# Feed-forward layer in two passes with a one-level Strassen input product

## The chip, the cores and the metric

The kernel runs on one core of a Trainium2 chip: TensorE (PE) for matrix products, VectorE (DVE), ScalarE (ACT) and GpSimd (POOL) for elementwise work, SyncE (SP) for issuing transfers between the off-chip memory and the on-chip buffers. The metric is the device time of one execution in microseconds (us), as the median of several runs.

## The reference

One layer of a hybrid diffusion backbone on 256 context tokens and 2048 latent tokens of width 1024, in float32. A mixing sublayer (differential attention, grouped-query attention, a bidirectional state-space scan) comes first, then a SwiGLU feed-forward sublayer; each ends in a layer norm. Only the second sublayer is changed. What matters of it:

```python
def swiglu(h, w_in, w_out):
    g, u = jnp.split(jnp.einsum('btd,df->btf', h, w_in), 2, axis=-1)
    return jnp.einsum('btf,fd->btd', jax.nn.silu(g) * u, w_out)
...
f = swiglu(x * (1 + scale2) + shift2, lp['w_ffn_in'], lp['w_ffn_out'])
x = layer_norm(ALPHA * x + gate2 * f, lp['ln_g'][1], lp['ln_b'][1])
```

The hidden width is 2816, which is 22 features of 128, each with a gate part g and an up part u.

## The kernel before

The stages run one after the other: modulation and input projections, state-space scans, attention, the output projection of the mixing sublayer (class `OutProj`), then the feed-forward layer (class `Ffn`, from L1536). For the engines PE, ACT, DVE and POOL, and in the last two stages for SP too, the order of the instructions is the order in which the program emits them. Every product is formed from operands split in two rounded parts, a high one and a low one (a float32r copy on ACT, the rest by a subtraction), as high x high + high x low + low x high: three matmuls for each 128 rows of the contraction.

`Ffn` works on three blocks of 768 tokens (18 tiles of 128). While the output projection does its last tiles, `inputs(0)` fetches and splits the first block's modulated rows, transposed, a 128-feature slice at a time (L1559 to L1565). For each block the 22 features go in four parts (`PARTS`). `hidden` forms a feature: for g, then for u, a piece of 128 x 1024 weights is loaded by SP (L1590), copied on ACT (L1593) and subtracted on POOL (L1594, the first ones on DVE), and for each half of 384 tokens 24 matmuls go into one bank (L1632 to L1634, tile pf). ACT takes the SiLU of g, DVE multiplies by u out of the bank, and ACT and DVE split the result into hh and hl (L1637 to L1640). After the features of a part, `out` multiplies them with their rows of the output weights, split by ACT and DVE (L1604, L1605), into six banks for each half of the 1024 columns (L1645 to L1647, tile fo), and `collect` adds the banks to facc (L1652, L1654). `normed` finishes a block beside the next block's features: gate on POOL (L1678), residual and statistics on DVE (L1680, L1683), scale on ACT (L1692), weight on DVE (L1693) and bias on POOL (L1695). The last part of the last block goes tile by tile (`last_out`, tile fl).

## Time and profile before

| what | value |
|---|---|
| median of 3 runs (lowest, highest) | 3869.7 us (3869.44, 3875.66) |
| the profiled execution: its span | 3868.3 us |
| mean granted TensorE clock | 0.974 of 2.4 GHz |
| busy DVE, ACT, POOL over the span | 2025.6, 1628.3, 1700.2 us |
| first matmul of the feed-forward stage, start | 2194.01 us |
| moved by DMA over the span | 318.67 MB, mean 82 GB/s |

The profiled execution is known by its span, from its first to its last instruction; the times of runs are those of the whole execution on the device. Durations of matmuls in a trace are modelled and overlap, so the distance between two starts is what one of them costs in a stream.

### The profile page before, as it was taken

To read this page: it belongs to the slowest core of one execution; us is meant where nothing else is said; L and a number is where in the kernel's file an instruction comes from. 1 tells how busy PE (TensorE), PEld (TensorE's weight loads), DVE (VectorE), ACT (ScalarE), POOL (GpSimd) and SP (SyncE) were. 2 spreads that over 40 slices of the span, in tenths; PEclk is the share of its full clock that TensorE was granted. 3 is DMA by queue.
4 is the path that set the end of the run, shared out by engine and by line. 5 is a ranking of instruction groups with operands and counts; after the bars stand their busy time and mean duration, and the time that the engine had idled before them with its cause. 6 is when DMAs were issued, how large, how long until landed. Compare 5 with 4: busy or idle time off the path is not lost.

```text
span 3868.3 us, 53596 instructions
## 1 busy us (share of the span) xinstructions
PE 3698.6 (96%) x20970; PEld 3006.8 (78%) x20970; DVE 2025.6 (52%) x3710; ACT 1628.3 (42%) x2802; POOL 1700.2 (44%) x1315
## 2 busy tenths in 40 slices
PE   6999899979999999999999999999999999999997
PEld 4878799965555554454478899999989999999996
DVE  3776666658888987667556521211611222611134
ACT  4555555538888883444434322122322122322212
POOL 3443267738888884445534422112422111611233
PEclk8999799989999999999999999999999999999999
DMA  5111244453310112011045511112321112311121
GB/s 195 46 52 39 91 128 124 122 163 117 88 39 20 42 39 65 14 33 36 14 161 178 181 63 68 66 58 72 129 91 60 68 64 97 133 60 58 68 101 52
DMA packets 214476, 318.67 MB, mean 82 GB/s; under 512 B 38632, under 2 KB 145032, under 8 KB 209616
## 3 DMA queue, kind: packets, MB, share of 16 engines
q1 hardware_dynamic: 194544, 295.49, 23.4%
q10 hardware_dynamic: 17232, 11.09, 1.0%
q0 software_dynamic: 2448, 8.67, 0.6%
q8 instruction: 165, 2.70, 0.3%
q14 instruction: 87, 0.71, 0.1%
HBM read 247.68 MB, written 67.52 MB: 81 GB/s over the span
## 4 chain that ended last, share of the span: by engine, by line
PE 46%; DVE 2%; POOL 1%; ACT 1%; issue 0%; DMA 0%; POOLq 0%; SPq 0%; ACTq 0%; DVEq 0%
PE pf L1634 9%; PE pf L1633 9%; PE pf L1632 9%; PE fo L1647 4%; PE fo L1646 4%; PE fo L1645 4%; PE opo L1440 2%; PE opo L1439 2%; PE opo L1438 2%; PE mpt L1430 0%; DVE facc L1680 0%; PE npt L1478 0%; POOL wi L1594 0%; DVE facc L1693 0%; DMA wir<-in_wfi 0%
## 5 line engine op out<-in xcount | busy, mean ns | idle before, releaser
L1594 POOL TENSOR_TENSOR wi<-wir,wi 128x1024 fp32r<-128x1024 f32 x128 | 313.7, 2451 | 1118.1 <-ACT wi L1593 1095.2
L1634 PE MATMUL pf<-fxh,wi 128*128 128x384 f32 x2112 | 708.3, 335 | 8.2 <-POOL wi L1594 6.9
L1632 PE MATMUL pf<-fxh,wi 128*128 128x384 f32 x2112 | 707.7, 335 | 1.3 <-ACT wi L1593 1.3
L1633 PE MATMUL pf<-fxl,wi 128*128 128x384 f32 x2112 | 707.5, 335 | 0.0
L1638 DVE TENSOR_TENSOR sg<-pf,sg 128x384 f32<-128x384 f32 x132 | 73.4, 556 | 768.2 <-PE pf L1634 761.5
L1176 DVE TENSOR_SCALAR_CACHE_REDUCE e<-ps 128x1024 f32<-128x1024 f32 (+1 forms) x384 | 393.1, 1040 | 66.2 <-PE ps L1171 64.5
L1634 PEld LDWEIGHTS pf<-fxh,wi 128*128 128x128 f32 x2112 | 397.9, 188 | 10.4 <-POOL wi L1594 8.5
L1632 PEld LDWEIGHTS pf<-fxh,wi 128*128 128x128 f32 x2112 | 398.0, 188 | 2.2 <-ACT wi L1593 1.7
L1633 PEld LDWEIGHTS pf<-fxl,wi 128*128 128x128 f32 x2112 | 397.8, 188 | 0.4
L1187 ACT ACTIVATE e<-e,nb 128x2560 f32<-128x2560 f32 x128 | 311.0, 2429 | 41.1 <-DVE nb L1181 41.1
L1593 ACT ACTIVATE wi<-wir 128x1024 fp32r<-128x1024 f32 x132 | 138.9, 1053 | 438.5 <-issue 341.8
L1209 POOL TENSOR_TENSOR e<-e,e 128x512 f32<-128x512 f32 x254 | 296.6, 1168 | 21.2
L1647 PE MATMUL fo<-wfh,hl 128*128 128x512 f32 x762 | 296.7, 389 | 0.0
L1646 PE MATMUL fo<-wfl,hh 128*128 128x512 f32 x762 | 296.6, 389 | 0.0
L1645 PE MATMUL fo<-wfh,hh 128*128 128x512 f32 x762 | 296.4, 389 | 0.0
L957 DVE TENSOR_REDUCE gmx<-gm 128x1 f32<-128x512 f32 (+1 forms) x304 | 214.2, 715 | 118.0 <-PE gm L956 115.5
L1171 PE MATMUL ps<-dk,dq 96*128 96x512 f32 x640 | 241.5, 460 | 28.8 <-DVE e L1176 16.8
L997 POOL TENSOR_TENSOR gag<-gag,ge 128x1024 f32<-128x1024 f32 x80 | 208.3, 2604 | 127.4 <-ACT ge L981 126.3
L1605 DVE TENSOR_TENSOR wfl<-wfr,wfh 128x512 fp32r<-128x512 f32 x127 | 90.2, 711 | 328.7 <-ACT wfh L1604 328.7
L981 ACT ACTIVATE ge<-gs 128x1024 f32<-128x1024 f32 x160 | 163.7, 1024 | 217.5 <-PE gs L979 213.5
L1639 ACT ACTIVATE hh<-sg 128x384 fp32r<-128x384 f32 x132 | 69.5, 526 | 433.7 <-DVE sg L1638 431.7
L1604 ACT ACTIVATE wfh<-wfr 128x512 fp32r<-128x512 f32 x127 | 79.9, 630 | 356.0 <-PE fo L1647 345.3
(433 smaller groups left out, 8088.3 us busy)
## 6 DMA issues: line engine op xcount, KB each, us to landing
wir<-in_wfi SPq DMA_DIRECT2D x132, 512.0 KB, 3.5
wfr<-in_wfo SPq DMA_DIRECT2D x132, 256.0 KB, 2.6
wada<-in_w_ada SPq DMA_DIRECT2D x24, 1024.0 KB, 7.2
yr<-in_xT SPq DMA_DIRECT2D x18, 512.0 KB, 3.8
stk_d<-sod SPq DMA_DIRECT2D x18, 512.0 KB, 3.4
mt<-mix_d SPq DMA_DIRECT2D x18, 512.0 KB, 4.8
xt<-in_xtok SPq DMA_DIRECT2D x18, 512.0 KB, 5.6
fxr<-x2T_d SPq DMA_DIRECT2D x24, 384.0 KB, 5.4
```

The costliest lines, as they stand in the source:

```text
L957: V.tensor_reduce(mx[:, 4 * r + q, i:i + 1], ps[:, 0:w], AX.X, ALU.max)
L1171: PE.matmul(ps[:, 512 * c:512 * c + 512], Q[0:96, m, qs], K[0:96, m, k0:k0 + 512], start=True, stop=True)
L1176: V.tensor_scalar(self.e[m][:, k0:k0 + w], ps[:, c:c + w], dscale, -3.4e38, ALU.mult, ALU.max, accum_out=mx[:, m, seen[m]:seen[m] + 1])
L1187: S.activation(self.e[m], self.e[m], AF.Exp, bias=self.nb[:, m:m + 1], accum_out=self.l[:, m:m + 1])
L1209: G.tensor_tensor(e0[:, a:b], e0[:, a:b], e1[:, a:b], ALU.add)
L1594: (G if f > 1 or blk else V).tensor_tensor(wl, raw, wh, ALU.subtract)
L1632: PE.matmul(o, wh[:, k], self.xh[:, k, cs], start=(k == 0), stop=False)
L1633: PE.matmul(o, wh[:, k], self.xl[:, k, cs], start=False, stop=False)
L1634: PE.matmul(o, wl[:, k], self.xh[:, k, cs], start=False, stop=(k == 7))
L1645: PE.matmul(po, hh[:, n, ts_], w[0], start=start, stop=False)
L1646: PE.matmul(po, hh[:, n, ts_], w[1], start=False, stop=False)
L1647: PE.matmul(po, hl[:, n, ts_], w[0], start=False, stop=stop)
```

## The change

The input product goes through all blocks first, and writes its result to memory (`h_d`, 22 x 128 x 2304); a second pass reads it back for the output product.

First pass (`first`), blocks of 768 tokens. The weights of a feature are a 2 x 2 matrix of blocks (g and u by two halves of the 1024 contraction rows), the tokens' rows another (two halves of the contraction by two halves of 384 tokens). Seven products of sums of such blocks, of four 128-row steps each, take the place of eight: products 1 (a, operand 11), 2 (a, 21), 5 (c, t1), 6 (d, t2), 7 (c, t3), 4 (b, t4), 3 (d, 22) in this order; t1 to t4 are the operand sums, c and d hold the weight sums. The sums that put the products together are formed on DVE from the banks and on POOL between SBUF tiles (`features`). Weight sums are formed on POOL in the first block (DVE for feature 0), stored in `ws_d` and loaded from there in the later blocks; a feature's weights are prepared beside the feature before it. The operand sums of the first block are formed on DVE (`start` beside the output projection, `rest` in feature 0), those of the later blocks on POOL beside the first block's features (`sums_of`, four sums a block), stored in `xc_d`. At a block's last feature the seven operands of the next are split (`inputs`).

Second pass (`second`): five groups of 4, 4, 4, 3 and 3 token tiles. For each group and each of the 22 features a piece holds 128 x 1024 output weights and the group's h (`pieces`), fetched three ahead and split by ACT and DVE into one of seven buffers; all 1024 columns of a tile accumulate over the 22 features in two banks. The last four features go tile by tile, and each tile is then gated, added to the residual and normalised (`added`, `normed`) beside the next group. The buffers of both passes are laid out anew; docstrings and comments are gone throughout. The core of the diff, added lines:

```diff
+        h_d = dram.tile([NF, 128, T], F32, name="h_d")
...
+            ffn = Ffn(tc, xp, I, x2T_d, h_d, dram)
...
+            op.run(ffn.start())
...
+TB, HB = 768, 384
+NB = T // TB
+SLOTS = ("11", "21", "t1", "t2", "t3", "t4", "22")
+RAWS = ("11", "12", "21", "22")
+BLOCKS = ((0, 4), (4, 4), (8, 4), (12, 3), (15, 3))
+NLAST = 4
...
+        self.ws_d = dram.tile([NF, 2, 128, 1024], F32, name="ws_d")
+        self.xc_d = dram.tile([NB - 1, 4, 128, 4 * HB], F32, name="xc_d")
+        self.raw, self.x, self.made = {}, {}, {}
+        f4 = lambda n, f: [(n, "g", I["wfi"][f, 0]), (n, "u", I["wfi"][f, 1])]
+        self.weights = [w for f in range(NF) for w in f4(f, f)]
+        for n in range(NF, NB * NF):
+            f = n % NF
+            self.weights += [(n, "a", I["wfi"][f, 0]), (n, "c", self.ws_d[f, 0]), (n, "d", self.ws_d[f, 1]),
+                             (n, "b", I["wfi"][f, 1][:, 512:1024])]
...
+        n, what, src = self.weights[self.nw]
+        q = self.nw % 4
+        r = self.made.pop(f"wq{q}", None)
+        if r is None:
+            pool = self.early if q < 2 else self.wr if q == 2 else self.wl
+            r = pool.tile([128, 2, 512], F32, name=f"wq{self.nw}", tag=f"wq{q}")
+        self.nw += 1
+        w = src.shape[1]
+        self.tc.nc.sync.dma_start(out=r.rearrange("p h c -> p (h c)")[:, 0:w], in_=src)
+        self.wraw[n, what] = r
...
+    def parts(self, key, at, blk, eng=None):
+        x = self.slot(f"fx{key}_{blk}", key)
+        s = self.raw[at].rearrange("p k t -> p (k t)")
+        self.tc.nc.scalar.activation(x[:, 0], s, AF.Copy)
+        (eng or self.tc.nc.vector).tensor_tensor(x[:, 1], s, x[:, 0], ALU.subtract)
+        self.x[key] = x.rearrange("p a (k t) -> p a k t", t=HB)
+
+    def combine(self, out, a, b, eng):
+
+        r = self.raw
+        eng.tensor_tensor(r[out], r[a], r[b], ALU.subtract)
...
+    def start(self):
+
+        V = self.tc.nc.vector
+        self.fetch(0, "11", "11")
+        self.fetch(0, "12", "12")
+        yield
+        self.parts("11", "11", 0)
+        yield
+        self.combine("11", "12", "11", V)
+        self.fetch(0, "21", "12")
+        yield
+        self.parts("t1", "11", 0)
+        yield
+        self.parts("21", "12", 0)
+        self.load_weights()
+        self.load_weights()
+        yield
+
+    def rest(self):
+
+        V = self.tc.nc.vector
+        self.parts("22", "22", 0)
+        yield
+        self.combine("11", "22", "11", V)
+        self.parts("t2", "11", 0)
+        yield
+        self.combine("22", "22", "21", V)
+        self.parts("t3", "22", 0)
+        yield
+        self.combine("12", "12", "11", V)
+        self.parts("t4", "12", 0)
+        yield
+
+    def sums_of(self, blk):
+
...
+        for at in RAWS:
+            self.fetch(blk, at, at)
+        yield
+        self.combine("11", "12", "11", G)
+        yield
+        store("11", 1)
...
+        for i in range(4):
+            self.fetch(blk, SLOTS[i], RAWS[i])
         yield
-        for k in range(8):
-            cur, raw = raw, fetch(k + 1) if k < 7 else None
-            nc.scalar.activation(self.xh[:, k], cur, AF.Copy)
-            nc.vector.tensor_tensor(self.xl[:, k], cur, self.xh[:, k], ALU.subtract)
-            yield
...
+        for key in ("22", "t2", "t3", "t4"):
+            made[f"x{key}"] = self.slot(f"fx{key}_0", key)
+        self.fetch(0, "12", "21")
+        self.fetch(0, "22", "22")
...
+            g, u = raw("g"), raw("u")
+            yield from split(n, "a", g)
+            yield from split(n, "b", u[:, 1:2])
+            eng.tensor_tensor(u[:, 1], u[:, 0], u[:, 1], ALU.add)
+            eng.tensor_tensor(u[:, 0], g[:, 0], u[:, 0], ALU.subtract)
+            yield
+            eng.tensor_tensor(g[:, 0], u[:, 1], g[:, 0], ALU.subtract)
+            eng.tensor_tensor(g[:, 1], g[:, 1], g[:, 0], ALU.subtract)
+            yield from split(n, "c", u)
+            yield from split(n, "d", g)
+            for r, s in ((u, 0), (g, 1)):
+                nc.sync.dma_start(out=self.ws_d[n, s], in_=r.rearrange("p h c -> p (h c)"))
+            self.load_weights()
+            self.load_weights()
...
+            for k in range(4):
+                cs = slice(128 * k, 128 * k + 128)
+                PE.matmul(o, w[:, 0, c, cs], x[:, 0, k], start=(k == 0), stop=False)
+                PE.matmul(o, w[:, 0, c, cs], x[:, 1, k], start=False, stop=False)
+                PE.matmul(o, w[:, 1, c, cs], x[:, 0, k], start=False, stop=(k == 3))
...
+            a1 = copy(n, "a1", product(n, 1, "a", 0, "11"))
+            yield
+            g0 = add(n, "g0", product(n, 2, "a", 1, "21"), a1)
+            S.activation(g0, g0, AF.Silu)
+            yield
+            a5 = copy(n, "a5", product(n, 5, "c", 1, "t1"))
+            if n == 0:
+                p3 = product(n, 3, "d", 1, "22")
+            yield
+            u2 = add(n, "u2", product(n, 6, "d", 0, "t2"), a1)
+            t = add(n, "t", u2, a5, G)
+            yield
+            u3 = add(n, "u3", product(n, 7, "c", 0, "t3"), u2)
+            up1 = add(n, "up", u3, a5, G)
+            yield
+            up0 = add(n, "u0", product(n, 4, "b", 0, "t4"), u3)
+            G.tensor_tensor(h[:, 0:HB], up0, g0, ALU.mult)
+            yield
+            g1 = add(n, "g1", p3 if n == 0 else product(n, 3, "d", 1, "22"), t)
+            S.activation(g1, g1, AF.Silu)
+            yield
+            V.tensor_tensor(h[:, HB:TB], up1, g1, ALU.mult)
+            nc.sync.dma_start(out=self.h_d[f, :, TB * blk:TB * blk + TB], in_=h)
+            for k in [k for k in W if k[0] <= n]:
+                W.pop(k)
+            yield
+
...
+        run(weights(0, V))
+        rest = self.rest()
+        next(rest)
+        next(rest)
+        before, side = iter(()), iter(())
...
+            prep = weights(n + 1, G) if n + 1 < N else iter(())
+            feats = features(n)
+            if f == NF - 5:
+                side = self.inputs(blk + 1) if blk + 1 < NB else self.pieces()
+                next(side)
+            for i in range(7):
+                next(feats)
+                if i == 0:
+                    run(before)
+                if n == 0 and i in (1, 2):
+                    next(rest)
+                if last and (blk + 1 < NB or i < 4):
+                    next(side)
+                next(prep, None)
+                if i in (0, 2, 3):
+                    next(prep, None)
+            run(prep)
+            if 2 <= n < NF - 5:
+                next(apart, None)
+            before = feats
...
+            r = raws[i] = self.rows([128, 1536], f"fo{b}_{f}", RAWS[i % 4])
+            nc.sync.dma_start(out=r[:, 0:1024], in_=self.I["wfo"][128 * f:128 * f + 128, :])
+            nc.sync.dma_start(out=r[:, 1024:1024 + 128 * n], in_=self.h_d[f, :, 128 * t:128 * t + 128 * n])
+
+        for i in range(3):
+            fetch(i)
+        yield
+        for i, (b, f) in enumerate(todo):
+            w = 1024 + 128 * BLOCKS[b][1]
+            r = raws.pop(i)
+            x = self.slot(f"fp{b}_{f}", SLOTS[i % 7])
+            nc.scalar.activation(x[:, 0, 0:w], r[:, 0:w], AF.Copy)
+            nc.vector.tensor_tensor(x[:, 1, 0:w], r[:, 0:w], x[:, 0, 0:w], ALU.subtract)
+            self.got[b, f] = x
+            if i + 3 < len(todo):
+                fetch(i + 3)
+            yield
+
...
+        po = {(0, t, h): bank(0, t, h) for t, h in order[2:] + order[:2]}
+
+        def piece(b, f, t, h):
+            x, o = self.got[b, f], po[b, t, h]
+            ts_ = slice(1024 + 128 * t, 1152 + 128 * t)
+            hs = slice(512 * h, 512 * h + 512)
+            PE.matmul(o, x[:, 0, ts_], x[:, 0, hs], start=(f == 0), stop=False)
+            PE.matmul(o, x[:, 0, ts_], x[:, 1, hs], start=False, stop=False)
+            PE.matmul(o, x[:, 1, ts_], x[:, 0, hs], start=False, stop=(f == NF - 1))
...
+            V.tensor_tensor(r[:, hs], po.pop((b, t, h)), gate[0 if ti < 2 else 1][:, hs], ALU.mult)
+            V.scalar_tensor_tensor(r[:, hs], x1s[ti][:, hs], ALPHA, r[:, hs], ALU.mult, ALU.add)
+            V.bn_stats(st[:, h], r[:, hs])
...
+            for f in range(NF - NLAST):
+                ready(b * NF + f + 2)
+                for t in range(n):
+                    for h in range(2):
+                        piece(b, f, t, h)
...
+                for h in range(2):
+                    for f in range(NF - NLAST, NF):
+                        piece(b, f, t, h)
+                    added(b, ti, t, h)
+                todo.append(normed(ti))
+                if last:
+                    run(todo.pop(0))
```

## Rows read from the trace of the kernel before

**Rows 1.** The page, busy time of each engine, share of the span, instructions.

```profile
PE 3698.6 (96%) x20970; PEld 3006.8 (78%) x20970; DVE 2025.6 (52%) x3710; ACT 1628.3 (42%) x2802; POOL 1700.2 (44%) x1315
```

**Rows 2.** The page, chain of waits: share of the span by line.

```profile
PE pf L1634 9%; PE pf L1633 9%; PE pf L1632 9%; PE fo L1647 4%; PE fo L1646 4%; PE fo L1645 4%; PE opo L1440 2%; PE opo L1439 2%; PE opo L1438 2%; PE mpt L1430 0%; DVE facc L1680 0%; PE npt L1478 0%; POOL wi L1594 0%; DVE facc L1693 0%; DMA wir<-in_wfi 0%
```

**Rows 3.** One tile's instructions (pf, fo, fl): count, duration ns min/median/max, starts.

```profile
L1632 PE MATMUL pf<-fxh,wi x2112: 333/334/688, 2194.0 to 3805.0; 128*128 128x384 f32 x192
...
L1645 PE MATMUL fo<-wfh,hh x762: 387/389/390, 2298.7 to 3825.3; 128*128 128x512 f32 x191
...
L1645 PE MATMUL fl<-fwh,hh x30: 389/389/389, 3826.0 to 3845.7; 128*128 128x512 f32 x30
```

**Rows 4.** Timeline of PE in steady stretches: start us, duration us, what ran.

```profile
2019.81 0.39 PE L1439 MATMUL opo<-wol,m 128*128 128x512 f32 x1
...
2023.54 0.39 PE L1440 MATMUL opo<-woh,m 128*128 128x512 f32 x1
...
2240.25 0.33 PE L1634 MATMUL pf<-fxh,wi 128*128 128x384 f32 x1
...
2243.37 0.33 PE L1634 MATMUL pf<-fxh,wi 128*128 128x384 f32 x1
...
2329.76 0.39 PE L1647 MATMUL fo<-wfh,hl 128*128 128x512 f32 x1
...
2342.45 0.39 PE L1646 MATMUL fo<-wfl,hh 128*128 128x512 f32 x1
```

**Rows 5.** Stretches: us, busy us by engine, granted clock, DMA share, GB/s.

```profile
1960.00:2180.00 220.00, 220.00 (x1085) 181.22 (x1084) 144.31 (x234) 95.78 (x220) 90.56 (x32) 1.00 0.51 170
...
2194.01:3846.50 1652.49, 1644.29 (x8712) 1548.71 (x8712) 437.42 (x628) 394.14 (x611) 431.27 (x192) 1.00 0.23 79
...
2760.00:2850.00 90.00, 87.18 (x492) 86.40 (x491) 44.56 (x53) 29.11 (x40) 52.96 (x25) 0.98 0.32 117
...
3310.00:3400.00 90.00, 85.89 (x492) 84.94 (x491) 52.99 (x53) 28.98 (x40) 53.90 (x26) 1.00 0.32 117
```

**Rows 6.** Timeline at the start of the feed-forward stage, PE, DVE and POOL.

```profile
2194.01 0.69 PE L1632 MATMUL pf<-fxh,wi 128*128 128x384 f32 x1 [1.33 <-ACT wi L1593]
...
2201.90 0.52 PE L1633 MATMUL pf<-fxl,wi 128*128 128x384 f32 x1
...
2202.46 0.34 PE L1632 MATMUL pf<-fxh,wi 128*128 128x384 f32 x1
...
2194.00 5.56 DVE L1594 TENSOR_TENSOR wi<-wir,wi 128x1024 fp32r<-128x1024 f32 x2
...
2195.23 3.24 POOL L1491 TENSOR_TENSOR r<-r,ln1b 128x1024 f32<-128x1024 f32 x1
```

**Rows 7.** Groups by line, feed-forward stage: busy us, mean ns | idle before, releasers.

```profile
L1564 DVE TENSOR_TENSOR fxl<-fxr,fxh 128x768 fp32r<-128x768 f32 x16 | 15.3, 957 | 0.6
...
L1593 ACT ACTIVATE wi<-wir 128x1024 fp32r<-128x1024 f32 x131 | 138.0, 1053 | 438.5 <-issue 341.8 <-DMA wir<-in_wfi 45.8 <-PE pf L1634 38.4
...
L1639 ACT ACTIVATE hh<-sg 128x384 fp32r<-128x384 f32 x132 | 69.5, 526 | 433.7 <-DVE sg L1638 431.7
```

**Rows 8.** One line's instructions on DVE or POOL: duration ns min/median/max, starts.

```profile
L1605 DVE TENSOR_TENSOR wfl<-wfr,wfh x127: 681/694/1698, 2284.0 to 3820.1; 128x512 fp32r<-128x512 f32 x127
...
L1638 DVE TENSOR_TENSOR sg<-pf,sg x132: 511/558/558, 2211.6 to 3805.8; 128x384 f32<-128x384 f32 x132
...
L1693 DVE TENSOR_TENSOR facc<-facc,ln2g x12: 1211/1964/3409, 2788.6 to 3355.6; 128x1024 f32<-128x1024 f32 x12
...
L1594 POOL TENSOR_TENSOR wi<-wir,wi x128: 2371/2400/3378, 2217.9 to 3782.0; 128x1024 fp32r<-128x1024 f32 x128
```

**Rows 9.** The page, DMA issues: count, KB each, us to landing.

```profile
wir<-in_wfi SPq DMA_DIRECT2D x132, 512.0 KB, 3.5
```

**Rows 10.** Stretches: the tail after the last matmul.

```profile
3846.50:3868.30 21.80, 0.04 (x1) 0.00 (x0) 16.46 (x26) 4.62 (x8) 10.79 (x5) 0.60 0.27 110
```

More of the change, by code (lines that the diff above doesn't have):

```diff
@@ L1565, in inputs, with run @@
             yield
-    def run(self, I, O, gates_d, x1_d, rstd_from, row_bc):
+    def run(self, O, gates_d, x1_d, rstd_from, row_bc):
+        tc = self.tc
+        self.late = self.lx.enter_context(tc.tile_pool(name="ffl", bufs=1, reuse_waits="tile"))
+        self.far = self.lx.enter_context(tc.tile_pool(name="ffr", bufs=1, side="right", reuse_waits="tile"))
+        with ExitStack() as wx:
+            self.first(wx)
+        with ExitStack() as wx:
+            self.second(O, gates_d, x1_d, rstd_from, row_bc, wx)
@@ L1568, in run, with first @@
+    def first(self, wx):
         tc = self.tc
@@ new lines, in first, with wtile @@
+        self.wr = wr = wx.enter_context(tc.tile_pool(name="ffw", bufs=1, side="right", reuse_waits="tile"))
+        self.wl = wl = wx.enter_context(tc.tile_pool(name="ffv", bufs=1, reuse_waits="tile"))
+        ps = wx.enter_context(tc.tile_pool(name="ffps", bufs=8, space=PSUM, reuse_waits="tile"))
+        N = NB * NF
+        W, made = {}, self.made
+        BLK = {"a": 2, "b": 1, "c": 2, "d": 2}
+        def wtile(n, what):
+            tag = f"w{what}{n % 2}"
+            t = made.pop(tag, None)
+            if t is None:
+                pool = wr if what == "a" or n % 2 == 0 else wl
+                t = pool.tile([128, 2, BLK[what], 512], F32R, name=f"w{what}_{n}", tag=tag)
+            return t
@@ new lines, in half, with inner @@
+        def half(n, what):
+            t = made.pop(what, None)
+            if t is None:
+                t = (wl if what == "g1" else wr).tile([128, HB], F32, name=f"f{what}_{n}", tag=what)
+            return t
+        def inner(n):
+            t = made.pop(f"h{n % 2}", None)
+            if t is None:
+                t = wl.tile([128, TB], F32, name=f"h_{n}", tag=f"h{n % 2}")
+            return t
+        for key in ("22", "t2", "t3", "t4"):
+            made[f"x{key}"] = self.slot(f"fx{key}_0", key)
@@ new lines, in first, with split @@
+        made["wq3"] = wl.tile([128, 2, 512], F32, name="wq3", tag="wq3")
+        made["wb1"] = wtile(1, "b")
+        for n in range(2):
+            made[f"h{n}"] = inner(n)
+        def split(n, what, src):
+            w = wtile(n, what)
+            v = lambda x: x.rearrange("p c d -> p (c d)")
+            s = v(src)
+            S.activation(v(w[:, 0]), s, AF.Copy)
+            yield
+            V.tensor_tensor(v(w[:, 1]), s, v(w[:, 0]), ALU.subtract)
+            W[n, what] = w
+            yield
@@ new lines, in weights @@
+        def weights(n, eng):
+            raw = lambda what: self.wraw.pop((n, what))
+            if n >= NF:
+                for what in "acdb":
+                    yield from split(n, what, raw(what)[:, 0:BLK[what]])
+                    self.load_weights()
+                return
+            g, u = raw("g"), raw("u")
[11 more added lines that the diff above has]
+            self.load_weights()
+            self.load_weights()
@@ new lines, in first, with pieces, fetch @@
+        self.ahead = side
+        run(before)
+    def pieces(self):
+        nc = self.tc.nc
+        todo = [(b, f) for b in range(len(BLOCKS)) for f in range(NF)]
+        raws, self.got = {}, {}
+        def fetch(i):
+            b, f = todo[i]
+            t, n = BLOCKS[b]
+            r = raws[i] = self.rows([128, 1536], f"fo{b}_{f}", RAWS[i % 4])
[3 more added lines that the diff above has]
+            fetch(i)
+        yield
+        for i, (b, f) in enumerate(todo):
[7 more added lines that the diff above has]
+                fetch(i + 3)
+            yield
```

375 lines of the change are left out of this document (147 added, 228 removed).

## The prediction

> **What bounds the kernel now.** I read the page's busy times first: TensorE is busy 96% of the span, the other engines about half [rows 1]. A busy PE is modelled, so the chain of waits comes next: the input product (tile pf, L1632 to L1634) holds 27% of the span and the output product (fo) 12%, all on PE [rows 2]. The counts are 3 x 2112 matmuls of 384 columns for pf and 3 x (762 + 30) of 512 for fo and fl [rows 3]. Their price is the distance between starts, not the listed duration: 18 pf matmuls take 3.12 us, 0.1733 each; 56 fo matmuls 12.69 us, 0.2267 each [rows 4]. 6336 x 0.1733 + 2376 x 0.2267 = 1098.1 + 538.6 = 1636.7 us, and the stage lasts 1652.5 (first pf to last fl), with PE idle for only 8.2 of it [rows 5]. So the stage is a matmul stream, and what counts is the number of matmuls and what interrupts them.
>
> **The change part by part**, against the profiled execution's own time (its span, 3868.3 us; the median of the runs shown is 1.4 higher, which I add at the end).
>
> 1. Fewer matmuls. A feature in a block of 768 tokens took 2 x 2 x 24 = 96 matmuls and takes 7 products x 12 = 84. Over 66 features that is 5544 instead of 6336; columns, operand types and the order high-high, high-low, low-high stay. 792 x 0.1733 = **-137.3 us**. The output product keeps 22 x 18 x 2 x 3 = 2376 matmuls of 512 columns: 0.
> The spacing is where the Trainium skill can be weighed ("TensorE: Matmul & The Clock Gate", Back-to-back issue gap). It gives columns / 2.4 + 2.5 ns, which is 162.5 ns for 384 columns, and the saving by it would be 128.7 us. The rows say 173.3, and I keep them.
>
> 2. Start of the feed-forward stage. Before, PE needed one weight piece to start; its 22nd matmul began at 2202.46, 8.45 us after the first, where 21 x 0.1733 = 3.6 were due (the first ones ran at the half clock: 384 columns at 1.2 GHz are 0.32): a loss of 4.8 [rows 6]. Now feature 0 needs four split weight matrices and operands t2, 22, t3, t4, all made in DVE's order after 2194.1. An SBUF-to-SBUF operation of 512, 768 and 1024 elements takes 0.69, 0.96 and 1.2 on DVE [rows 7, 8], so one of 1536 takes 1.9. DVE's queue up to the last product: splits a, b, c, d (1.2 + 0.7 + 1.2 + 1.2), four weight sums (2.8), the split of 22 and three combine-and-split pairs (7 x 1.9 = 13.3), the next split a and g0 (1.8): 22.2 us. Beside it POOL finishes the last rows' affine steps, four operations of 2.4; there DVE's two splits took 5.56 instead of 2.4, because each stood behind one of POOL's [rows 6, 8]. I add 9 for that, and 5 for DVE waiting on ScalarE's copies (1.6 each) between combine and split. So operand t4 is ready near 2230, its product ends near 2232, and 14.6 were due: a loss of 24, and 1 more for half clock. 25 - 4.8 = **+20 us**. Bounds: 22.2 + 2.1 - 14.6 = 10 (+5) if POOL and ScalarE never hold DVE, 35 (+30) if every product also runs 12 x 0.32 = 3.8.
>
> 3. First block, steady state. A feature lasts 84 x 0.1733 = 14.56 us on PE. ScalarE: copies of 3584 elements (3.8) and four of 384 (2.1) [rows 7]. DVE: splits of 3584 elements (4.3), one product of SBUF operands (0.56), five sums that read PSUM (2.8). POOL, by 2.37 for 1024 elements [rows 8]: four weight sums of 512 (4.7), three operations of 384 (2.7), and in eight features one operand sum of 1536 for a later block (3.6). By order of issue, the c and d splits for the next feature end about 11.6 and 16.1 us into this one, and are wanted at 18.7 and 20.8. **+2**, bounds 0 to 53 (first rival).
> Transfers: 1 MB of weights in, 1 MB of sums and 0.4 MB of h out, about 165 GB/s; the output-projection stage moved 170 with PE never idle [rows 5]. SP issues all of it in order. A store of h waits for the end of the feature and holds the weight loads behind it; they are due a feature later and land in 3.5 us [rows 9]: 0, and 3.5 us a feature if that lead were gone.
>
> 4. Block changes. Seven operands are split in the last feature of a block (ScalarE +11, DVE +7.6, POOL +11), each after the product that frees its buffer. Following the queues, t4 comes 3.4 and t2 0.8 late: 4.3 a change, 9 in all. Before, the two changes cost 2.8 and 4.1 of idle PE and some clock, with POOL in both [rows 5]: about 11 with all else that the old stage lost behind its start (1652.5 - 1636.7 - 4.8). I take **0**, bounds -11 to +14.
>
> 5. Second pass. Each of 110 pieces (22 features, five token groups) costs ScalarE 1.6 and DVE 1.9, against 24 x 0.2267 = 5.44 us of PE (4.08 in the groups of three tiles), and 720 to 786 KB: 144 to 176 GB/s, with residual rows and results 210. Three are fetched ahead, so one may take 12 us to land. The DVE and ScalarE work that goes (facc, the hidden halves) lay beside matmuls: 0. Entering the pass costs **+2** (bounds 0 and 10): the banks are taken in the order in which the last feature frees them.
>
> 6. The side steps in the output projection: three ScalarE copies and four DVE operations of 1536 instead of eight each of 768, 5 against 6.6 and 7.6 against 7.7, where PE is busy throughout and DVE 144 of 220 [rows 5]: 0, and 7.6 if PE did not cover it.
>
> 7. Tail. 21.8 us now [rows 10], DVE working off tiles 3 to 5. The last group has 24 matmuls a tile (5.4 us) and some 9 of DVE, so the backlog is about 10, then gate, statistics and the last write: near 20. **-2**, bounds -6 (a backlog of 6) and +3 (one more DVE operation held by POOL).
>
> Sum: -137.3 + 20 + 2 + 0 + 2 + 0 - 2 = -115.3; 3753.0, and with the 1.4 of the median **3754 us**.
>
> **Rivals.**
> A. The first block is held by DVE against POOL. In the trace a DVE operation with two SBUF inputs takes 1.21 alone and up to 3.41 beside POOL, a POOL one 2.37 up to 3.38, while one that reads PSUM never exceeds 0.56 [rows 8]. In the eight features with an operand sum the two need 4.9 + 11 = 15.9 of 14.56: +11 over the eight; if one POOL operation of 2.4 lands on the path of every feature, 22 x 2.4 = +53. So 3765 to 3807. Against it: most waits end long before PE wants the operand. The Trainium skill ("SBUF — State Buffer", Who interferes with whom) calls the shared port an exclusive lock for the whole instruction; the trace agrees (3.41 against 1.21). By that rule the 15.9 cannot be shortened by overlap, and this change adds work on both sides of it.
> B. Matmuls space out. The output projection's 512-column matmuls stand 0.2333 apart (16 in 3.73 us) where fo has 0.2267 [rows 4], for no reason that the trace names; if the new buffers have it too, 7920 x 0.0067 = +53: 3807.
> C. The second pass waits for transfers: at 150 GB/s a group of three would take 4.8 per piece, +0.72 x 44 = +32: 3786. Against it: 170 GB/s over the projection stage [rows 5].
> D. Slower than before. If the stalls of the first block recur in every feature, PE may stay at 1.2 GHz, as it did for 8 us after the idle stretch at 2194 [rows 6]: 84 x (0.32 - 0.1733) = 12.3 us a feature. It decides from 9.4 such features on; all 22 give +271: 4025. Against it: the POOL waits at the second block change left the granted clock at 1.00 [rows 5].
> E. The start loses only its lower bound (-15), and the first block and the entry to the second pass nothing (-4): 3735.
>
> **How the numbers follow.** Forecast (3740 to 3770) 0.68; A 0.12; B 0.06; C 0.04; D 0.04; E 0.06. The likeliest gives 3754. The range takes in E, the bounds of the start and most of A: 3735 to 3800, with B's and D's upper ends left out. 0.2% is 8 us, what a measurement of this kernel can tell from no change: faster 0.95, same 0.01, slower 0.04.
>
> **What would show it.** 5544 product matmuls at 0.173 and 2376 at 0.227; the end of feature 0 some 38 us after its first matmul, DVE full and waits on t3 and t4; in the first block PE without gaps and DVE splits of up to 3.5 us; short gaps at two block changes, named by POOL; PE solid in the second pass at DMA near 0.5. A spacing near 0.180, PE gaps in each feature of the first block, or a granted clock below 0.95 outside the start would make it wrong.

## The result and the profile after

The changed kernel takes 3807.96 us (median of 4 runs, 3802.97 to 3815.84), the kernel before 3872.68 beside it; the ratio is 0.9825, 95% interval [0.9805, 0.9846]. So it is faster, by 65 us where 116 were forecast, and the time lies above the range (3735 to 3800).

The sums below are made on the two profiled executions (span 3868.3 before, 3804.0 after). Single executions differ ahead of the feed-forward stage, where the code differs in little but the side steps beside the output projection: the stage's first matmul starts between 2193.96 and 2207.02 us in the profiles of this study. I therefore compare *stage lengths*, from the first product matmul to the end of the span: 1674.3 before (3868.3 - 2194.01), 1608.0 after.

The page after, its line of busy times, which answers to [rows 1], and the head of its chain of waits, which answers to [rows 2]:

```profile
PE 3597.9 (95%) x20178; PEld 2887.0 (76%) x20178; DVE 2488.1 (65%) x4100; ACT 1786.4 (47%) x2890; POOL 1761.7 (46%) x1440
...
PE f L1785 5%; PE f L1786 5%; PE f L1784 5%; PE fy L1925 5%; PE fy L1923 5%; PE fy L1924 5%; POOL fxt L1607 0%; DMA wq<-in_wfi 0%; POOL fx L1607 0%; DVE fr L1936 0%; ACT fx L1606 0%; DVE fst L1937 0%; DVE fr L1935 0%; ACT fr L1951 0%; DVE wa L1749 0%
```

PE has 792 instructions fewer (20970 to 20178), as counted. Stretches after, which answer to [rows 5] and [rows 10] (columns as there): feature 0; features 1 to 21, the rest of the first block; the two later blocks; the second pass; the tail:

```profile
2195.96:2231.53 35.57, 23.70 (x84) 21.03 (x85) 29.63 (x20) 12.44 (x13) 12.85 (x8) 0.74 0.31 113
2231.53:2582.97 351.44, 320.89 (x1765) 309.10 (x1765) 204.72 (x209) 115.17 (x169) 221.31 (x154) 0.99 0.54 196
2582.97:3243.00 660.03, 651.34 (x3698) 649.77 (x3698) 357.94 (x452) 253.54 (x369) 209.46 (x139) 0.99 0.49 165
3243.00:3782.90 539.90, 539.90 (x2376) 445.75 (x2375) 307.55 (x339) 175.88 (x156) 55.25 (x19) 1.00 0.53 184
3782.90:3804.00 21.10, 0.39 (x2) 0.00 (x0) 14.10 (x27) 2.73 (x6) 5.25 (x3) 0.62 0.17 66
```

A feature is due 84 x 0.1733 = 14.56 us. Features 1 to 21 are due 305.8 and take 351.4: here 45.7 us are lost. And none of the engines that feed PE is full in that stretch: DVE is busy 204.72 of 351.44 us, ACT 115, POOL 221. Who is waited for, PE's waits of the stage (total us, times, longest):

```profile
PE f L1786 <- DVE wd L1749: 26.1, 21, 1.3
PE f L1785 <- POOL fxt L1607: 7.2, 2, 5.2
PE f L1786 <- DVE wc L1749: 6.0, 8, 2.9
```

In each of the 21 features PE stops for the split of d, the weight sum that products 6 and 3 read: 0.85 to 1.33 us, 1.24 on average. It is the gap in each feature of the first block that the prediction named as a sign of being wrong. This wait has no counterpart in [rows 5], where PE was idle for 8.2 us in 1652.

**The round.** The timeline of one feature of the first block after, by engine (start, duration, what ran, idle time before it and its releaser). It shows one full round, from POOL's L1768 to the next, 2503.29 - 2487.05 = 16.24 us later; plain features of this block (those that no operand sum on POOL delays), from the third on, last 16.2 to 16.3:

```profile
2487.05 1.29 POOL L1768 TENSOR_TENSOR wq<-wq,wq 128x512 f32<-128x512 f32 x1
2488.43 2.16 POOL L1769 TENSOR_TENSOR wq<-wq 128x512 f32<-128x512 f32 x1
...
2499.70 1.29 POOL L1765 TENSOR_TENSOR wq<-wq 128x512 f32<-128x512 f32 x1 [7.16 <-DVE wb L1749]
2501.07 1.29 POOL L1766 TENSOR_TENSOR wq<-wq,wq 128x512 f32<-128x512 f32 x1
2502.32 1.02 POOL L1791 TENSOR_TENSOR ft<-fu,fa 128x384 f32<-128x384 f32 x1
2503.29 1.30 POOL L1768 TENSOR_TENSOR wq<-wq,wq 128x512 f32<-128x512 f32 x1
...
2490.62 1.06 ACT L1747 ACTIVATE wd<-wq 128x1024 fp32r<-128x1024 f32 x1 [3.40 <-POOL wq L1769]
2494.18 0.53 ACT L1822 ACTIVATE fg<-fg 128x384 f32<-128x384 f32 x1 [2.50 <-DVE fg L1791]
2494.61 0.47 ACT L1796 ACTIVATE fa<-f 128x384 f32<-128x384 f32 x1
2494.98 1.05 ACT L1747 ACTIVATE wa<-wq 128x1024 fp32r<-128x1024 f32 x1
2497.85 0.53 ACT L1806 ACTIVATE fg<-fg 128x384 f32<-128x384 f32 x1 [1.82 <-DVE fg L1791]
2498.28 0.62 ACT L1747 ACTIVATE wb<-wq 128x512 fp32r<-128x512 f32 x1
...
2491.71 1.91 DVE L1749 TENSOR_TENSOR wd<-wq,wd 128x1024 fp32r<-128x1024 f32 x1 [1.16 <-ACT wd L1747]
2493.55 0.54 DVE L1791 TENSOR_TENSOR fg<-f,ft 128x384 f32<-128x384 f32 x1
2496.06 1.22 DVE L1749 TENSOR_TENSOR wa<-wq,wa 128x1024 fp32r<-128x1024 f32 x1 [0.71 <-ACT wa L1747]
2497.21 0.55 DVE L1791 TENSOR_TENSOR fg<-f,fa 128x384 f32<-128x384 f32 x1
2498.93 0.69 DVE L1749 TENSOR_TENSOR wb<-wq,wb 128x512 fp32r<-128x512 f32 x1 [1.17 <-ACT wb L1747]
...
2493.68 0.45 PE L1786 MATMUL f<-fxt,wd 128*128 128x384 f32 x1 [1.25 <-DVE wd L1749]
```

Read it in order of time. POOL ends the last weight sum of feature n at 2490.59; ACT copies d at 2490.62; DVE splits it at 2491.71, to 2493.62, and PE goes on at 2493.68. Behind that split, in DVE's order, stands g1 of feature n-1, whose product was done before (2493.55, no wait of its own). Behind g1 stands its SiLU on ACT (2494.18); behind this, in ACT's order, the copy of a for feature n+1 (2494.98); then DVE's split of a (2496.06), then g0, its SiLU, the copy of b (2498.28) and the split of b (2498.93), and only then may POOL overwrite u with the weight sums of feature n+1 (2499.70, after 7.16 us in which it did nothing). Every link starts within 0.1 us of the end of the one before. Few of them need each other's data: a, b and the sums belong to a later feature than g1 and g0. They are tied by their place in two queues, and the chain closes on itself. Its length sets the pace: 16.24 against PE's 14.6 to 14.8.

### The profile page after: what moved, and what is told of

Read it like the earlier page. It is cut to its first block, busy times and chain, and to the rows that moved or that the text cites. A ratio compares the mean times of both kernels' runs of the same rounds, so it can differ in the third digit from the quotient of the medians.

```text
span 3804.0 us, 53881 instructions
## 1 busy us (share of the span) xinstructions
PE 3597.9 (95%) x20178; PEld 2887.0 (76%) x20178; DVE 2488.1 (65%) x4100; ACT 1786.4 (47%) x2890; POOL 1761.7 (46%) x1440
## 5 line engine op out<-in xcount | busy, mean ns | idle before, releaser
L1925 PE MATMUL fy<-fp 128*128 128x512 f32 x792 | 308.8, 390 | 0.0
L1923 PE MATMUL fy<-fp 128*128 128x512 f32 x792 | 308.7, 390 | 0.0
L1924 PE MATMUL fy<-fp 128*128 128x512 f32 x792 | 308.5, 389 | 0.0
L1887 DVE TENSOR_TENSOR fp<-fo,fp 128x1536 fp32r<-128x1536 f32 (+1 forms) x110 | 208.4, 1908 | 141.5 <-ACT fp L1886 126.5
L1791 POOL TENSOR_TENSOR ft<-fu,fa 128x384 f32<-128x384 f32 x66 | 104.2, 1579 | 404.4 <-DVE fu L1791 370.9
L1174 PE MATMUL ps<-dk,dq 96*128 96x512 f32 x640 | 242.5, 462 | 29.1 <-DVE e L1179 16.8
L1886 ACT ACTIVATE fp<-fo 128x1536 fp32r<-128x1536 f32 (+1 forms) x110 | 157.4, 1443 | 193.4 <-PE fy L1925 174.0
L1211 POOL TENSOR_SCALAR e<-e,c 128x512 f32<-128x512 f32 x254 | 182.2, 717 | 108.5 <-DVE c L1203 98.7
L1224 ACT ACTIVATE wT<-pt 128x512 f32<-128x512 f32 x320 | 178.4, 590 | 63.7 <-PE pt L1223 63.0
L1234 PE MATMUL po<-wT,vl 128*64 128x256 f32 x1280 | 203.2, 405 | 0.0
L1223 PEld LDWEIGHTS pt<-cst,e 128*128 128x128 f32 x1280 | 159.1, 141 | 57.2 <-POOL e L1212 13.3
L1223 PE MATMUL pt<-cst,e 128*128 128x128 f32 x1280 | 195.7, 275 | 5.6 <-POOL e L1212 3.6
L225 PE MATMUL px<-xhTrue,wx 128*128 128x260 f32 (+2 forms) x864 | 181.6, 303 | 14.4 <-DVE l L374 7.0
```

Of the source, the lines that this page charges most:

```text
L1174: PE.matmul(ps[:, 512 * c:512 * c + 512], Q[0:96, m, qs], K[0:96, m, k0:k0 + 512], start=True, stop=True)
L1223: PE.transpose(pt[:, k], self.e[0][:, 128 * (4 * g + k):128 * (4 * g + k) + 128], ident)
L1234: PE.matmul(po[64 * e:64 * e + 64], hd.v[:, k + e], self.wT[:, k + e], start=(k == 0), stop=(k == NKT - 2))
L1887: nc.vector.tensor_tensor(x[:, 1, 0:w], r[:, 0:w], x[:, 0, 0:w], ALU.subtract)
L1923: PE.matmul(o, x[:, 0, ts_], x[:, 0, hs], start=(f == 0), stop=False)
L1924: PE.matmul(o, x[:, 0, ts_], x[:, 1, hs], start=False, stop=False)
```

## The experiments

The theory that they test is this closed chain: the expectations call it Q, or the round theory. Its rival, there P or port, is my own rival A: DVE and POOL hold each other off, so that their load, whatever its order, is what the first block lasts. The table gives what the profiles show, in us: the stage length, feature 0, features 1 to 21 together (305.8 due), the plain features among them and the eight that an operand sum can delay (features 1 and 2, and a feature right behind a long one, aside), and the first features of the second and third block (14.56 due). The 42 other features take 617.5 in all but two kernels (617.9 and 619.1). Each row is one profiled execution.

| kernel | stage | feature 0 | 1 to 21 | plain | with operand sum | block 2, 3 |
|---|---|---|---|---|---|---|
| changed | 1608.0 | 35.57 | 351.4 | 16.2 to 16.3 | 17.4 to 17.5, two of 19.1, behind each one of 15.8 to 15.9 | 23.73, 18.75 |
| b first | 1579.2 | 37.27 | 320.6 | 14.6 to 14.8 | 16.2 to 16.4, one of 14.8 | 24.01, 18.76 |
| no operand sums | 1598.6 | 35.59 | 341.9 | 16.2 to 16.3 | 16.2 to 16.3 | 23.80, 18.75 |
| extra sum, off the chain | 1619.8 | 37.22 | 361.3 | 16.2 to 16.3 | 17.0 to 20.1 | 23.99, 18.71 |
| the same, b first | 1590.4 | 38.79 | 330.1 | 14.6 to 14.8 | 16.3 to 17.5 | 24.15, 18.72 |
| extra sum, on the chain | 1637.5 | 35.60 | 380.1 | 17.5 to 17.7, two of 19.2 | 17.2 to 20.6 | 24.56, 18.74 |
| the same, b first | 1589.8 | 38.05 | 330.6 | 14.6 to 15.2 | 15.3 to 18.4 | 23.93, 18.73 |
| weight sums on DVE | 1566.3 | 35.61 | 314.6 | 14.6 to 14.8 | 14.6 to 16.0 | 18.73, 18.74 |
| up and h on DVE | 1618.1 | 35.60 | 354.5 | 15.7 to 15.9 | 15.8 to 19.9 | 26.34, 21.16 |
| b first, operand sums on DVE | 1569.6 | 35.59 | 312.8 | 14.6 to 14.8 | 14.9 to 15.2 | 23.82, 18.72 |
| operand splits on DVE | 1605.9 | 35.57 | 351.7 | 16.2 to 16.3 | 17.4 to 17.5 | 22.93, 16.71 |
| the three edits together | 1565.3 | 37.26 | 311.2 | 14.6 to 14.8 | 14.6 to 15.2 | 21.52, 16.70 |
| no last affine | 1601.6 | 29.26 | 349.7 | 16.2 to 16.3 | 17.4 to 17.5 | 24.80, 18.74 |

**1. Order alone: b ahead of a.** Nothing is taken away, no operation changes its engine; the split of b, which POOL waits for, stands before that of a.

```diff
-            yield from split(n, "a", g)
             yield from split(n, "b", u[:, 1:2])
+            yield from split(n, "a", g)
```

> One pair of lines swapped: in the first block the split of b stands ahead of that of a. The work on every engine, and what DVE and POOL ask of their common port, is the same. Theory Q (a closed chain through the in-order queues: weight sums on POOL, copy and split of d, g1, SiLU, copy a1, copy and split of a, g0, SiLU, copy and split of b, the next weight sums; 16.24 us a round in the trace after, PE waits for it): the stretch from the copy of a to the copy of b, 3.3 us, leaves the chain, which is then 12.9 and shorter than PE's 14.6; plain features of the first block go from 16.2 to about 14.7, the whole from 3808 to 3768-3778. Theory P (the port shared by DVE and POOL is what a feature lasts, my rival A): no work leaves the port, features stay at 16 to 16.3, the whole within 5 of 3808.

Measured: 3784.2 us (3783.09 to 3787.38; 0.9759 [0.9742, 0.9776] of before), stage 28.8 us shorter than the change's. The first block, features 1 to 21:

```profile
2240.36:2560.95 320.59, 311.42 (x1765) 308.10 (x1765) 191.70 (x207) 114.42 (x168) 218.95 (x153) 1.00 0.59 213
```

POOL is busy 218.95 us, as before the edit (221.31), in a block that is 31 us shorter. Plain features run at PE's pace. That is what Q says. The swap also lets the two engines meet less: DVE is busy 13.0 us less than in the change (191.70 against 204.72). That is 0.6 us a feature, where each plain feature became 1.5 shorter, so it does not account for the gain by itself. It came out 6 us above the expected range: seven operand-sum features kept 1.6 over the others, and feature 0 cost 1.7 more. The work that PE waits for was not later: in both kernels its last wait of feature 0 ends 33.6 us after its first matmul. But here the matmuls behind that wait start 0.32 us apart, at a granted clock of 0.50 (2236.67 to 2240.04); with b first and the operand sums on DVE (35.59 in the table) they do not, though the wait ends at the same place. What decides it is not shown.

**2. Without the operand sums.** POOL's four sums per later block are left out (the later blocks then multiply other operands).

```diff
-        self.combine("11", "12", "11", G)
...
-        self.combine("21", "21", "22", G)
```

> Leaves out the eight operand sums that POOL forms for the later blocks in the first one (their transfers to and from memory stay, so the later blocks compute with unsummed rows). Q and P: the features that last 17.4 and 19.1 us fall to the 16.2 of the plain ones, since a DVE product of two SBUF operands stands behind the 3.6 us sum; -9 to -11, near 3798. A third account, that the 0.8 MB transfers in SP's queue hold those features: they stay at 17.4 and 19.1, and the whole at 3808.

Measured: 3798.3; features 1 to 21 fall by 9.5 to 341.9, and from the third on every one lasts 16.2 to 16.3. The operand sums are a second, smaller loss on top of the round. The trace of the changed kernel shows how, in feature 5, by POOL's and DVE's timeline:

```profile
2305.31 4.45 POOL L1613 TENSOR_TENSOR fr<-fr,fr 128x1536 f32<-128x1536 f32 x1
...
2307.62 2.57 DVE L1824 TENSOR_TENSOR h<-fup,fg 128x384 f32<-128x384 f32 x1 [0.71 <-issue]
```

The product h takes DVE 0.56 in other features and 2.57 here, to 0.43 past the end of POOL's sum (2309.76), and it stands ahead of the split of a: the round is 1.2 longer.

**3. One more sum on POOL, off the chain and on it.** Off: an extra 512-element sum ahead of the weight sums. On: the same sum between them, reading the new u.

```diff
+            if eng is G:
+                G.tensor_tensor(wl.tile([128, 512], F32, name=f"xt_{n}", tag="xt"), u[:, 0], u[:, 1], ALU.add)
             eng.tensor_tensor(u[:, 1], u[:, 0], u[:, 1], ALU.add)
+            if eng is G:
+                G.tensor_tensor(wl.tile([128, 512], F32, name=f"xt_{n}", tag="xt"), u[:, 0], u[:, 1], ALU.add)
             eng.tensor_tensor(u[:, 0], g[:, 0], u[:, 0], ALU.subtract)
```

(The first pair of lines is the first kernel, the second pair the second. The sum goes to a tile that nothing reads; what the third expectation says of the output is mistaken.)

> One more POOL sum of 512 elements (1.3 us, its result unused) ahead of the weight sums of every feature of the first block, the order of splits as in the changed kernel. Q: it lies on the closed chain, plain features go from 16.24 to 17.4-17.7, +26 to +30 in all, near 3835. If the period came from PE, from the transfers or from a queue with room: 16.24, 3808.

> The same extra POOL sum, with b split ahead of a as in e1. Q: the chain is 12.9 + 1.3 = 14.2, still under PE's 14.7, so plain features stay at 14.6-14.8 and only the eight with an operand sum, which the port holds, grow by about 1.3: 3784 to 3796. P (a feature lasts what the port is asked for, wherever it stands in the order): every feature grows by about 1.3, near 3812.

> The changed kernel with one more 512-element GpSimd sum per feature of the first block, placed between the two u sums and reading the new u (it computes the same u again from the value just made, so the weights of the second sum differ: that part of the output is changed). It stands inside the round that I take for the bound, where the one before stood in GpSimd's idle gap. Round theory (weight sums, split of d, SiLU, splits of a and b, next weight sums form one closed chain): plain features go from 16.24 to about 17.5 us (+1.29), the whole to about 3808 + 21 x 1.29 = 3835 us. Rival (port or some other capacity bounds the first block, GpSimd has room): plain features stay at 16.2 to 16.4.

> The same extra sum, with the split of b ahead of that of a. Round theory: the round, some 12.9 us long with b first, grows to 14.2 and stays under TensorE's 14.7, so plain features stay at 14.6 to 14.9 us; operand-sum features go to 17.4 to 17.8; the whole 3784 to 3798 us. Rival (the extra operation costs what it costs wherever it stands): plain features 15.9, the whole about 3811.

The first expectation was wrong, and in a telling way. The whole took 3827.81, where 3835 was expected from longer plain features; but those did not change (16.2 to 16.3). The stage began 10.2 us later in this execution, and the 9.9 that features 1 to 21 took more lie in the operand-sum features. POOL's timeline, extra sum off the chain, shows that I had put it beside the chain: it doesn't wait for the split of b, and ran in POOL's idle stretch right behind h.

```profile
2513.96 2.27 POOL L1766 TENSOR_TENSOR xt<-wq 128x512 f32<-128x512 f32 x1
2521.22 1.29 POOL L1767 TENSOR_TENSOR wq<-wq 128x512 f32<-128x512 f32 x1 [4.99 <-issue]
```

It took 2.27 us of POOL in every plain feature at no cost in time, which P does not allow. The same sum put on the chain (POOL's timeline):

```profile
2529.63 1.29 POOL L1765 TENSOR_TENSOR wq<-wq 128x512 f32<-128x512 f32 x1 [7.17 <-DVE wb L1749]
2531.01 1.29 POOL L1767 TENSOR_TENSOR xt<-wq 128x512 f32<-128x512 f32 x1
...
2547.23 1.29 POOL L1765 TENSOR_TENSOR wq<-wq 128x512 f32<-128x512 f32 x1 [7.17 <-DVE wb L1749]
```

The whole took 3843.43 (near 3835 expected; the stage is 29.5 longer than the change's). The round is 2547.23 - 2529.63 = 17.60 us, 1.36 longer, which is the extra sum's place (2532.38 - 2531.01 = 1.37), while POOL still idles for 7.17 us. With b first the off-chain sum again leaves plain features alone (3792.57, within the expected range), and the on-chain one takes them to 15.1 to 15.2 (3790.34, within the range for the whole; the features are 0.3 over). There the second u sum takes 2.15 beside DVE's split of a: 0.86 more than I had counted. In a plain feature the same operation thus costs 0, 1.36 or about 0.5 us by where it stands.

**4. Weight sums on DVE, order as in the change.**

```diff
-            prep = weights(n + 1, G) if n + 1 < N else iter(())
+            prep = weights(n + 1, V) if n + 1 < N else iter(())
```

> The changed kernel with the weight sums of the first block on VectorE in GpSimd's place, order of a and b as in the change. Round theory: the sums take less time there and no lock, the round shortens from 16.2 by some 3 to 4 us to below TensorE's 14.7: plain features 14.6 to 15.0 us, the whole 3770 to 3785 us. Rival (VectorE is the bound of the first block): plain features get longer than 16.3 by VectorE's added 4 to 5 us, the whole about 3900.

Measured: 3766.88 (one run), better than expected. The sums on DVE's timeline:

```profile
2498.52 0.69 DVE L1749 TENSOR_TENSOR wb<-wq,wb 128x512 fp32r<-128x512 f32 x1 [1.17 <-ACT wb L1747]
2499.25 0.69 DVE L1765 TENSOR_TENSOR wq<-wq 128x512 f32<-128x512 f32 x1
2499.98 0.69 DVE L1766 TENSOR_TENSOR wq<-wq,wq 128x512 f32<-128x512 f32 x1
...
2501.77 1.39 DVE L1769 TENSOR_TENSOR wq<-wq 128x512 f32<-128x512 f32 x1
...
2505.34 1.66 DVE L1749 TENSOR_TENSOR wd<-wq,wd 128x1024 fp32r<-128x1024 f32 x1
```

From the end of b's split to the end of the last sum there are 3.95 us (2499.21 to 2503.16) where POOL took 7.2 (2499.62 to 2506.82). DVE is now busy 256 us of 315, where the change has 205 of 351, and the block is 37 us shorter: DVE's load was not the bound. It also shortened the first change of blocks by 5.0, which I had not expected. A likely reason, not tested by itself, is the start of the splits: ACT begins to copy the next block's operands 2.7 us into the last feature (2537.14 - 2534.41), against 7.6 in the kernel with b first (2553.91 - 2546.32), since d no longer comes late in its own feature.

**5. Sum u + a5 and product h on DVE** (L1816, L1819).

```diff
-            up1 = add(n, "up", u3, a5, G)
+            up1 = add(n, "up", u3, a5)
-            G.tensor_tensor(h[:, 0:HB], up0, g0, ALU.mult)
+            V.tensor_tensor(h[:, 0:HB], up0, g0, ALU.mult)
```

> The sum up and the product h of the first half go from POOL to DVE in every feature: POOL has 2.0 us less, DVE 1.1 more, and the split of d no longer stands behind POOL (1.9 us, 1.2 alone). Q: the chain loses that wait and gains nothing, plain features of the first block go from 16.24 to 15.4-15.7, -12 to -17 over the block, near 3794. P: the port's sum falls by 2.0 - 0.9, features to about 15.1, near 3784. If the locks lie off the chain: 16.2, 3808.

Missed: 3814.01. Both operations now stand ahead of the split of d in DVE's order, that is, on the round. The timeline of DVE:

```profile
2540.99 1.07 DVE L1791 TENSOR_TENSOR fup<-fu,fa 128x384 f32<-128x384 f32 x1
...
2542.56 0.56 DVE L1819 TENSOR_TENSOR h<-fu,fg 128x384 f32<-128x384 f32 x1
2543.03 1.22 DVE L1749 TENSOR_TENSOR wd<-wq,wd 128x1024 fp32r<-128x1024 f32 x1
```

Freed of POOL, the split of d takes 1.22 where it took 1.91; but it starts 0.30 behind d's copy where it started 0.03 behind, and plain features gain only 0.4. The operand-sum features give back more than that (up to 19.9; features 1 to 21 are 3.1 longer in all), and the changes of blocks add 5.0 (26.34 and 21.16).

**6. Operand sums, and operand splits at the changes, on DVE; the best version.** The first kernel has b first and the operand sums on DVE, the second the operand splits alone, the third all three edits.

```diff
-        G, nc = self.tc.nc.gpsimd, self.tc.nc
+        G, nc = self.tc.nc.vector, self.tc.nc
...
-            self.parts(key, RAWS[i % 4], blk, nc.gpsimd if i % 2 else nc.vector)
+            self.parts(key, RAWS[i % 4], blk, nc.vector)
```

> Two of the three edits of e8, the splits of a block change left as they are (three of seven on POOL): tells the operand sums apart from the block changes. Q with the port: the eight features at 14.7-15.2, the block changes at 24 and 18.8 as in e1, 3771-3776. Transfers as the cause: the eight at 16.3, 3784.

> At a block change all seven operands are split on DVE, where three were POOL's. If POOL's place in the chain is the cause (t4 split there takes 4.9 us with the lock, after t waits for t2): the features at the block changes fall from 23.7 and 18.8 to 15-17, -8 to -12 in all, near 3798. If the landing of the raw rows is the cause: they stay within 1 us, near 3808. If DVE (seven splits of 1.8 beside 7.7 us of its own) becomes the bound: above 24.

> Three edits: b split ahead of a (as e1), the later blocks' operand sums formed on DVE instead of POOL, and all operands of a block change split on DVE (as e3). In e1 the eight features with an operand sum still last 16.3, where DVE (4.9) and POOL (8.2 + 3.5) ask 16.6 of the common port. Theory Q + port in those eight: on DVE the sum takes 1.8, the port is asked for 14.9, the eight features fall to 14.7-15.2 (-9 to -13), and the block changes, which no longer start late, to 15-19 (-6 to -10): 3762-3772. If the eight features are held by the transfers of the rows instead: only the block changes fall, 3774-3780. If DVE becomes the bound: not under 3784.

The first, 3778.65, takes 7.8 off features 1 to 21 beside b first alone, so the operand sums' loss went with POOL; its whole is 3 over the range. The second missed: 3806.84; the changes gained 0.8 and 2.0, the seven splits now standing one behind the other on DVE. Together, five runs: **3763.14 us (3762.09 to 3774.38), 0.9727 [0.9714, 0.9741]** of before, faster than both kernels; by stage length it is 1.0 ahead of the weight sums on DVE, one run there, which is less than feature 0 alone differs between profiles. Its first block, features 1 to 21, with PE busy throughout:

```profile
2232.29:2543.49 311.20, 310.46 (x1766) 308.65 (x1766) 188.37 (x216) 114.42 (x168) 183.26 (x144) 1.00 0.61 220
```

**7. The start, without POOL's last affine steps.**

```diff
-                    G.tensor_tensor(r, r, g_bc, ALU.mult)
-                    G.tensor_tensor(r, r, b_bc, ALU.add)
+                    if not end:
+                        G.tensor_tensor(r, r, g_bc, ALU.mult)
+                        G.tensor_tensor(r, r, b_bc, ALU.add)
```

> The changed kernel without GpSimd's affine of the last two tiles of the input at the start of the layer (that part of the computation is left out). If GpSimd's queue and the lock with VectorE there make the first feature late, feature 0 goes from 35.6 to 28 to 30 us and the whole to 3800 to 3802 us; if the first feature waits for its weights or for the chain of its own splits, feature 0 stays at 35 to 36 and the whole at 3808.

Measured: feature 0 falls from 35.57 to 29.26, within what POOL and the lock as the cause let expect; the stage from 1608.0 to 1601.6. The whole, 3805.16, hides it, as this execution's stage began 5.9 us later (2201.82). DVE and POOL at the start in the changed kernel, timeline:

```profile
2198.11 2.85 DVE L1749 TENSOR_TENSOR wb<-wq,wb 128x512 fp32r<-128x512 f32 x1
...
2201.72 3.46 DVE L1766 TENSOR_TENSOR wq<-wq,wq 128x512 f32<-128x512 f32 x1
2205.22 2.73 DVE L1768 TENSOR_TENSOR wq<-wq,wq 128x512 f32<-128x512 f32 x1
...
2197.17 3.24 POOL L1494 TENSOR_TENSOR r<-r,ln1b 128x1024 f32<-128x1024 f32 x1
...
2202.23 2.39 POOL L1493 TENSOR_TENSOR r<-r,ln1g 128x1024 f32<-128x1024 f32 x1
```

and in the kernel without the affine steps:

```profile
2202.94 0.69 DVE L1750 TENSOR_TENSOR wb<-wq,wb 128x512 fp32r<-128x512 f32 x1
...
2204.39 0.69 DVE L1767 TENSOR_TENSOR wq<-wq,wq 128x512 f32<-128x512 f32 x1
2205.12 0.69 DVE L1769 TENSOR_TENSOR wq<-wq,wq 128x512 f32<-128x512 f32 x1
```

The three operations take 2.1 us and took 9.0.

## Why the prediction was right or wrong

By its points, each against the stage of the profiled execution:

| point | predicted | measured | from |
|---|---|---|---|
| 1 fewer matmuls | -137.3 | -137.3 | 792 fewer, at 0.1733 |
| 2 start | +20 | +16.2 | 35.57 - 14.56 = 21.0, less 4.8 before |
| 3 first block | +2 | **+45.7** | 351.4 - 305.8 |
| 4 changes of blocks | 0 | +2.4 | 23.73 + 18.75 - 29.1 = 13.4, less 11 |
| the later features | 0 | +6.0 | 617.5 - 42 x 14.56 = 617.5 - 611.5 |
| 5 second pass | +2 | +1.3 | 539.9 - 538.6 |
| 7 tail (6 lies ahead of the stage) | -2 | -0.7 | 21.1 - 21.8 |
| sum | -115.3 | -66.4 | 1608.0 - 1674.3 = -66.3, the same but for rounding |

**The step that failed is point 3**, 43.7 of the 49 us by which the sum was short, and in it the sentence "By order of issue, the c and d splits for the next feature end about 11.6 and 16.1 us into this one, and are wanted at 18.7 and 20.8". In the trace the feature with product 6 at 2491.91 began 36 matmuls earlier, near 2485.6, the one before it 16.24 earlier; so the split of d, over at 2493.62, ends 24.3 us into the feature before, 8.2 later than I had it, and PE, which needs it from the third matmul of product 6 on, waits 1.25 us. I followed the queues once, from a feature's start at which all engines were free, and found a lead of 4.7 us. But the steps of that walk end behind each other's next turn: d's split of this feature is ahead of g1 of the last, this ahead of a and b of the next, these ahead of the next sums. A walk through one turn shows whether a chain is late; only the length of the closed turn shows the pace that it settles at, and a lead of 4.7 us would be used up by an excess of 1.7 in three features. The round's durations add up: four POOL weight sums 6.04, POOL's sum of 384 1.02, copies of d, a and b 2.73, their splits 3.82, g1 and g0 1.09, two SiLUs 1.06, a copy of 384 0.47, together 16.23. Most of these were in [rows 7, 8], and their order in the code.

**Rival A** had the size, if barely (3765 to 3807, chance 0.12; measured 3807.96), and part of the mechanism. The lock is in the round: POOL's L1769 takes 2.16 where 1.29 is its time alone, DVE's split of d 1.91 where 1.22 is, together 1.56 of the 16.24; without it the round would be near 14.7, PE's own pace. But A's "one POOL operation on the path of every feature" is not what sets the time: an operation more on POOL cost a plain feature nothing off the chain, and another order of two splits took 28.8 us away with every operation in place, of which, by their busy times, DVE held up less can be 13.0 and POOL 2.4. What the lock by itself is worth was not tried, since each edit that removes it moves an operation too. The Trainium skill ("SBUF — State Buffer", Who interferes with whom) was the rule that A weighed, an exclusive lock for the whole instruction; the start agrees: DVE's split of b, begun at 2198.11 beside POOL's L1494 (2197.17 to 2200.41), ends at 2200.96, 0.55 after it, where it takes 0.69 alone.

**The other points.** In point 2 the terms held: the lock was put at 9, and the DVE operations that met POOL (the first splits of a and b, L1766 and L1768) were 8.0 longer than alone (2.24, 2.85, 3.46 and 2.73 against 1.22 and three of 0.69), DVE's waits for ScalarE's copies 4.8 for 5; operations of 1536 took 1.75, not 1.9. Point 4 was the right size by luck as much as by working: I had t4 3.4 us late and t2 0.8, but t4 was never late, t2 was by 5.16 at the first change and 2.09 at the second, and operand 21 by 1.22 at the first. POOL and PE at the first change:

```profile
2583.11 3.49 POOL L1607 TENSOR_TENSOR fx<-fr,fx 128x1536 fp32r<-128x1536 f32 x1 [9.40 <-ACT fx L1606]
...
2591.78 4.93 POOL L1607 TENSOR_TENSOR fxt<-fr_1t,fxt 128x1536 fp32r<-128x1536 f32 x1
...
2596.76 0.69 PE L1785 MATMUL f<-fxt,wd 128*128 128x384 f32 x1 [5.16 <-POOL fxt L1607]
```

The last POOL line is the split of t2, product 6's operand. It began only at 2591.78, behind a sum for which POOL had waited 3.37 us for DVE, and took 4.93 where POOL's split before it took 3.49. With the splits on DVE, which gained only 0.8 here, PE waits in five places, 0.3 to 1.5 us each, for DVE and ACT. **Rival B**, matmuls further apart, came in small: of the later features every second takes 14.63, the others 14.78, against 14.56. **Rival C** fell: PE is busy for all 539.9 us of the second pass at 184 GB/s. **Rival D** fell: with 1.24 us of wait in every feature the granted clock of the first block is 0.99. **Rival E** fell with point 3. The range failed with it: I had 53 as the bound of point 3 from A, and gave A too small a chance because I took "most waits end long before PE wants the operand" from the single walk.

## What to carry to other kernels

Where work for the next turn of a loop shares in-order queues with work for this one, look for the cycle that leads from a step through the queues back to the same step one turn later, and add up its durations: that is a bound as hard as an engine's busy time, and it can hold with every engine in it under two thirds busy. What shortened it here was the order at its links, or an operation moved off it; work on an idle engine beside it cost nothing in the plain features, though not in those where another operation filled the idle stretch. To find it in a trace, start at the wait that recurs every turn and go back by releaser and by queue place until you meet the same line again.
